# A bidirectional hybrid encoder: a fourth seven-product pair per gate/up group, and half of the lower weight halves made by accumulating DMA

## The chip, the cores and the metric

One core of a Trainium2 chip runs the whole kernel in one launch. The metric is device time in microseconds, the median of three runs; lower is better. A profiled execution of the same program gives the page and the trace.

## The reference

Two layers over 256 tokens of width 2048, in float32. Each layer mixes tokens (layer 0 by a chunked gating unit, layer 1 by grouped-query attention with a 2-D rotary embedding), attends to 256 memory tokens, and then runs a dense SwiGLU feed-forward network of width 5632:

```python
x = x + jnp.concatenate([tok_out, mem_out], axis=-1) @ w_out[l]
x = x + swiglu(rms_norm(x, g_ffn[l]), w_gate_up[l], w_down[l])

def swiglu(h, w_gate_up, w_down):
    gate, up = jnp.split(h @ w_gate_up, 2, axis=-1)
    return (jax.nn.silu(gate) * up) @ w_down
```

The gate/up weights are 2 x 2048 x 11264 numbers, the down weights 2 x 5632 x 2048. All weights are read once from HBM.

## The kernel before, in words

**Three matmuls for one product.** Every operand is split into a rounded upper half and the remainder, both in the type fp32r. A product is three matmuls (`matmul3`, L185 to L189): upper x upper, lower x upper, upper x lower. Each has 128 x 128 stationary numbers (activations, turned) and 128 x 512 moving ones (weights), and adds into a PSUM bank.

**Splitting the weights.** A raw tile (tag `raw`, four slots, 128 x 4 x 512, 1 MB) comes in by two transfers of 512 KB from SyncE's queue. `halves` (L265) makes from it `whi` by a cast on ScalarE (L271) and `wlo` = raw - whi on VectorE (L272). There are three slots each of `whi` and `wlo`.

**Groups and pairs.** The gate/up projection of a layer goes in 11 groups of 512 gate and 512 up columns (class `Pair`, L333). A group takes two column blocks (gate, up) by two blocks of 128 tokens, and walks through the 2048 rows in eight pairs of 128-row blocks. An ordinary pair (`eight`, L409) makes eight products, 24 matmuls. A fast pair (`seven`, L395) gets the same result from seven products, 21 matmuls, in the manner of Strassen and Winograd: sums of activations are made once per layer (`feature_sums`), and sums of weights for each pair in `prepare` (L362): the tile `T` of three blocks by L371 and L373, and one block of `raw` overwritten by L372. `T` then goes through `halves` as well (L397, 128 x 1536). Products 1, 5, 6, 7 add up in four banks of their own (`banks2`), the others in four `acc` banks. After the last fast pair `inner` (L421) evicts the four special banks to a tile `E` (L425 to L428). After the last pair `outer` (L443) adds the `acc` banks to it, and lines 845 to 850 do the SiLU gating and send the result through a transposing DMA (L200 to L206) to the down projection. Groups come in chunks of four, four and three; each is followed by its part of the down projection, which uses the same class with fast pairs of its own.

**What sets the order.** `run` (L350) prepares each pair one ahead, also across the groups of a chunk; `tick` puts due side work in between. The order on each engine is then set by a scheduler from the order of the code and from slots coming free, and each engine runs its list strictly in that order. In the first group of a layer two pairs are fast, in the other ten three. Hence a group has 6 x 24 + 2 x 21 = 186 or 5 x 24 + 3 x 21 = 183 matmuls.

Of the kernel before, what the change touches and what calls it, by code (L numbers as in the profile page):

```python
# [10 lines left out]
F32 = mybir.dt.float32  # L11
# [6 lines left out]
P = 128  # L18
# [13 lines left out]
KC2 = 2  # L32
KC4 = 4
MIX_TILES = 36
FFN_TILES = 26
W_TILES = 3
RAW_TILES = 4
KC3 = 3
# [3 lines left out]
class Parts:  # L42
# [8 lines left out]
    def get(self, kc, t):  # L51
        return self.ap[kc, t]
# [3 lines left out]
def encoder(ctx: ExitStack, tc: tile.TileContext, x, x_t, mem, mem_t, columns, w_in_a, g_v_a, spatial_t, w_in_b,  # L56
# [128 lines left out]
    def matmul3(out, a, b, start, stop):  # L185

        nc.tensor.matmul(out, lhsT=a[0], rhs=b[0], start=start, stop=False)  # L187
        nc.tensor.matmul(out, lhsT=a[1], rhs=b[0], start=False, stop=False)  # L188
        nc.tensor.matmul(out, lhsT=a[0], rhs=b[1], start=False, stop=stop)  # L189
# [75 lines left out]
    def halves(raw, n, step=KC4):  # L265

        hi = wp.tile([P, KC4, NB], F32R, tag="whi", name=nm("whi"))[:, :n]
        lo = wp.tile([P, KC4, NB], F32R, tag="wlo", name=nm("wlo"))[:, :n]
        for c in range(0, n, step):
            cut = slice(c, min(c + step, n))  # L270
            nc.scalar.copy(hi[:, cut], raw[:, cut])  # L271
            nc.vector.tensor_tensor(lo[:, cut], raw[:, cut], hi[:, cut].bitcast(F32), ALU.subtract)  # L272
# [60 lines left out]
    class Pair:  # L333
# [1 line left out]

        def __init__(self, parts, sums, w, na, nb, order, fast, into=None):
            self.parts, self.sums, self.w, self.na, self.nb, self.into = parts, sums, w, na, nb, into  # L340
            self.bank, self.two, self.part, self.ready = {}, {}, {}, {}
            self.order, self.fast = order, fast
# [19 lines left out]
        def prepare(self, i):  # L362
# [5 lines left out]
            if i in self.fast:  # L368
# [4 lines left out]
                nc.vector.tensor_tensor(T[:, 2], raw[:, 0], raw[:, 2], ALU.add)  # L373
                self.ready[i] = raw, T

        def fetch(self, i):
            raw = wp.tile([P, KC4, NB], F32, tag="raw", name=nm("raw"), bufs=RAW_TILES)
            rows = slice(2 * i * P, (2 * i + 2) * P)
            for cut, n0 in ((slice(1, 3), self.na), (slice(0, 4, 3), self.nb)):
                nc.sync.dma_start(raw[:, cut], self.w[rows, n0:n0 + NB].rearrange("(c p) n -> p c n", p=P))  # L380
            return raw

        def add(self, name, a, b):
# [7 lines left out]
            self.part.setdefault(name, 0)  # L391
            self.part[name] += 1
            matmul3(self.bank[name], a, b, self.part[name] == 1, self.part[name] == self.of.get(name, self.most))

        def seven(self, i, raw, T):  # L395
            t2, w00, w10, w11 = halves(raw, KC4)
            t1, t3, t4 = halves(T, KC3)  # L397
            get, (q5, s2, q7, q3) = self.parts.get, self.sums[i]
            k0, k1 = 2 * i, 2 * i + 1
            inner = [(1, get(k0, 0), w00), (6, s2, t2), (5, q5, t1), (7, q7, t3)]  # L400
            outer = [(2, get(k1, 0), w10), (3, q3, w11), (4, get(k1, 1), t4)]
            if self.bank:
                inner, outer = inner[:2] + outer[:2], inner[2:] + outer[2:]
            for some in (inner, outer):
                for name, a, b in some:
                    self.add(name, a, b)
                tick()

        def eight(self, i, raw):  # L409
            done = i == self.order[-1]  # L410
            w01, w00, w10, w11 = halves(raw, 4)
            get, k0, k1 = self.parts.get, 2 * i, 2 * i + 1
            for t, names in ((0, (2, 3)), (1, (4, 8))):
                for name, pair in zip(names, ((w00, w10), (w01, w11))):
                    self.add(name, get(k0, t), pair[0])
                    self.add(name, get(k1, t), pair[1])
                if done:
                    self.outer(t)
                tick()

        def inner(self):  # L421

            b = self.bank
            E = room["p"].tile([P, 4, NB], F32, tag="e", name=nm("e"), bufs=1)
            nc.scalar.copy(E[:, 0], b[1])  # L425
            nc.vector.tensor_tensor(E[:, 3], b[6], E[:, 0], ALU.subtract)
            nc.vector.tensor_tensor(E[:, 1:3], self.two[5, 7], E[:, 3:].to_broadcast([P, 2, NB]), ALU.add)
            nc.vector.tensor_tensor(E[:, 3], b[5], E[:, 2], ALU.add)  # L428
            if self.into:
                for t in range(NT):  # L430
                    later(1 + t, lambda t=t: self.add_inner(E, t))
            self.out = self.into or [[E[:, 2 * t + n] for n in range(2)] for t in range(NT)]
# [7 lines left out]
            else:  # L440
                nc.vector.tensor_tensor(o.whole, o.whole, E[:, :2], ALU.add)

        def outer(self, t):  # L443

            o = self.out
            for n, name in enumerate(((2, 3), (4, 8))[t]):
# [201 lines left out]
    for l in range(DEPTH):  # L648
# [172 lines left out]
        for chunk in (range(0, 4), range(4, 8), range(8, 11)):  # L821
# [103 lines left out]
```

## Time and profile before

| | |
|---|---|
| median of 3 runs (range) | 1997.43 us (1996.91 to 1998.39) |
| profiled execution, its own time | 2000.43 us |
| its span | 1998.7 us |
| TensorE busy | 1987.4 us (99%), clock granted 1.0 |
| VectorE busy | 1595.2 us (80%) |
| ScalarE busy | 1228.9 us (61%) |
| GpSimd busy | 66.4 us (3%) |
| bytes by DMA | 416.48 MB, mean 208 GB/s |

The engines are PE (TensorE matmul), PEld (its weight loads), DVE (VectorE), ACT (ScalarE), POOL (GpSimd) and SP (SyncE, which only issues transfers). A row of instructions gives line, engine, operation, output <- inputs, shapes and count; then busy time in us and the mean ns of one; then the idle time of the engine before them and what ended it. A row of waits gives total us, times and the longest. In the DMA rows a digit is the busy tenths of the 16 DMA engines in one slice of the window, and below it stand the GB/s of the slice. The queue q1 carries SyncE's transfers, q10 those of ScalarE (the transposes), q0 those of GpSimd.

### The profile page before, as it was taken

What the parts mean: (1) busy time and instruction counts of PE and PEld (TensorE: products, weight loads), DVE (VectorE), ACT (ScalarE), POOL (GpSimd) and SP (SyncE); (2) the same over time, 40 slices, a digit from 0 to 9 for tenths busy, and PEclk for the clock granted to TensorE, in tenths of its full rate; (3) what the DMA queues carried; (4) which work ended last, traced back from release to release, by engine and by line L of the source; (5) the groups of instructions that cost most, each with busy time, mean ns of one, the idle gap of its engine ahead of it and who ended that gap; (6) DMA issues with size and microseconds to landing.
All of it is one profiled execution on the core that took longest, in us unless ns stands there. A gap on an engine that the chain in (4) does not pass through costs nothing.

```text
span 1998.7 us, 23974 instructions
## 1 busy us (share of the span) xinstructions
PE 1987.4 (99%) x8956; PEld 1646.0 (82%) x8956; DVE 1595.2 (80%) x1700; ACT 1228.9 (61%) x1476; POOL 66.4 (3%) x106
## 2 busy tenths in 40 slices
PE   9999999999999999999999999999999999999998
PEld 7888888888888878888888888888888888888887
DVE  6665568998888979886666886699988899888887
ACT  8757775676446764466765765756754466644673
POOL 2200001000000000000011000010000000000000
PEclk9999999999999999999999999999999999999999
DMA  9856875676656877657766434757866567765674
GB/s 352 296 187 179 242 212 188 190 231 216 220 197 183 229 201 229 205 184 232 228 219 201 162 129 158 219 180 207 241 205 212 188 206 213 225 219 190 199 220 139
DMA packets 276965, 416.48 MB, mean 208 GB/s; under 512 B 85200, under 2 KB 85456, under 8 KB 276848
## 3 DMA queue, kind: packets, MB, share of 16 engines
q1 hardware_dynamic: 199808, 387.62, 59.6%
q10 hardware_dynamic: 74352, 18.81, 5.8%
q0 software_dynamic: 2688, 8.52, 1.4%
q8 instruction: 70, 1.15, 0.2%
q14 instruction: 47, 0.39, 0.1%
HBM read 394.45 MB, written 2.10 MB: 198 GB/s over the span
## 4 chain that ended last, share of the span: by engine, by line
PE 89%; DVE 4%; DMA 3%; issue 2%; ACT 2%; SPq 0%; ACTq 0%; DVEq 0%
PE acc L189 26%; PE acc L187 26%; PE acc L188 26%; PE m L189 4%; PE m L187 4%; PE m L188 4%; DVE wlo L272 2%; DMA a<-a 1%; ACT whi L271 1%; DMA raw<-in_w_down 1%; DMA raw<-in_w_in_a 1%; PE m L193 1%; DVE T L371 0%; DVE e L448 0%; PE m L542 0%
## 5 line engine op out<-in xcount | busy, mean ns | idle before, releaser
L272 DVE TENSOR_TENSOR wlo<-raw,whi 128x2048 fp32r<-128x2048 f32 (+2 forms) x466 | 840.4, 1819 | 253.1 <-ACT whi L271 235.5
L271 ACT CAST whi<-raw 128x2048 fp32r<-128x2048 f32 (+2 forms) x466 | 705.6, 1535 | 428.5 <-PE acc L188 316.4
L187 PE MATMUL acc<-whi,h 128*128 128x512 f32 x1440 | 561.4, 390 | 0.8 <-ACT whi L271 0.8
L188 PE MATMUL acc<-whi,h 128*128 128x512 f32 x1440 | 561.0, 390 | 0.0
L189 PE MATMUL acc<-wlo,h 128*128 128x512 f32 x1440 | 516.0, 391 | 0.7 <-DVE wlo L272 0.6
L187 PE MATMUL acc<-whi,a 128*128 128x512 f32 x1052 | 410.0, 390 | 3.3 <-DVE x L448 2.1
L188 PE MATMUL acc<-whi,a 128*128 128x512 f32 x1052 | 410.0, 390 | 0.0
L189 PE MATMUL acc<-wlo,a 128*128 128x512 f32 x1052 | 394.4, 390 | 0.2 <-DVE wlo L272 0.2
L189 PEld LDWEIGHTS acc<-wlo,h 128*128 128x128 f32 x1440 | 270.4, 188 | 59.6 <-DVE wlo L272 4.1
L187 PEld LDWEIGHTS acc<-whi,h 128*128 128x128 f32 x1440 | 270.4, 188 | 56.5 <-ACT whi L271 1.5
L188 PEld LDWEIGHTS acc<-whi,h 128*128 128x128 f32 x1440 | 270.4, 188 | 55.7
L187 PEld LDWEIGHTS acc<-whi,a 128*128 128x128 f32 x1052 | 197.6, 188 | 44.7 <-issue 2.5
L189 PEld LDWEIGHTS acc<-wlo,a 128*128 128x128 f32 x1052 | 197.6, 188 | 42.3 <-DVE wlo L272 1.7
L188 PEld LDWEIGHTS acc<-whi,a 128*128 128x128 f32 x1052 | 197.6, 188 | 40.5
L271 ACT CAST whi<-T 128x1536 fp32r<-128x1536 f32 x84 | 124.4, 1481 | 96.3 <-PE acc L188 75.9
L272 DVE TENSOR_TENSOR wlo<-T,whi 128x1536 fp32r<-128x1536 f32 x84 | 146.9, 1749 | 0.0
L371 DVE TENSOR_TENSOR T<-raw 128x1024 f32<-128x1024 f32 x84 | 102.3, 1217 | 26.0 <-DMA raw<-in_w_gate_up 24.0
L189 PE MATMUL m<-wlo,a 128*128 128x512 f32 x272 | 106.1, 390 | 0.2 <-DVE wlo L272 0.2
L187 PE MATMUL m<-whi,a 128*128 128x512 f32 x272 | 106.0, 390 | 0.2 <-ACT whi L271 0.2
L188 PE MATMUL m<-whi,a 128*128 128x512 f32 x272 | 105.9, 389 | 0.0
L206 ACT COPY sg<-a 128x1024 uint16<-128x1024 uint16 x44 | 51.6, 1174 | 54.9 <-DMA a<-a 54.7
L200 ACT COPY a<-sg 128x1024 uint16<-128x1024 uint16 x44 | 45.9, 1044 | 26.0 <-issue 13.2
(122 smaller groups left out, 1474.7 us busy)
## 6 DMA issues: line engine op xcount, KB each, us to landing
raw<-in_w_gate_up SPq DMA_DIRECT2D x352, 512.0 KB, 4.7
raw<-in_w_down SPq DMA_DIRECT2D x176, 512.0 KB, 5.0
raw<-in_w_out SPq DMA_DIRECT2D x32, 1024.0 KB, 5.3
raw<-in_w_in_a SPq DMA_DIRECT2D x24, 1024.0 KB, 6.9
raw<-in_w_in_b SPq DMA_DIRECT2D x24, 1024.0 KB, 5.2
raw<-in_w_mem_kv SPq DMA_DIRECT2D x16, 1024.0 KB, 5.2
a<-in_mem_t POOLq DMA_DIRECT2D x16, 256.0 KB, 3.9
raw<-in_w_in_a SPq DMA_DIRECT2D x7, 512.0 KB, 8.1
```

Source lines behind the costliest of these rows:

```text
L187: nc.tensor.matmul(out, lhsT=a[0], rhs=b[0], start=start, stop=False)
L188: nc.tensor.matmul(out, lhsT=a[1], rhs=b[0], start=False, stop=False)
L189: nc.tensor.matmul(out, lhsT=a[0], rhs=b[1], start=False, stop=stop)
L193: nc.tensor.transpose(dst[:, c * P:(c + 1) * P], src[:, c * P:(c + 1) * P], ident)
L200: nc.scalar.copy(planes.rearrange("p (h n) -> p h n", h=2), src.bitcast(U16).rearrange("p (n h) -> p h n", h=2))
L206: nc.scalar.copy(halves, back.rearrange("p (h n) -> p n h", h=2))
L271: nc.scalar.copy(hi[:, cut], raw[:, cut])
L272: nc.vector.tensor_tensor(lo[:, cut], raw[:, cut], hi[:, cut].bitcast(F32), ALU.subtract)
L371: nc.vector.tensor_tensor(T[:, :2], raw[:, 1:4:2], w01, ALU.add)
```

## The change

In the ten later gate/up groups of each layer four pairs are fast instead of three, in the order 0, 4, 1, 2, 5, 3, 6, 7 (fast: 0 to 3). In all 22 gate/up groups half of each raw tile gets its lower halves in another way (`added`): ScalarE casts the raw blocks to `whi` (L388) and writes their rounded negation to `wlo` (L389), and a DMA issued by GpSimd adds the raw numbers to that (L390). In a fast pair the source is the raw tile in SBUF, in an ordinary pair it is HBM once more. The other half goes the old way, in instructions of half the size. The matmuls that need the accumulated halves are put last in their pair (`late`). `E` loses its own buffer and takes one of the four raw slots; the memory goes to the pool of activations (26 to 30 tiles), which holds the sums of the fourth pair. The down projection has the new place of `E` but no accumulating DMA.

```diff
-FFN_TILES = 26
+FFN_TILES = 30
...
         def fetch(self, i):
             raw = wp.tile([P, KC4, NB], F32, tag="raw", name=nm("raw"), bufs=RAW_TILES)
...
+            apart = i in self.fast or not self.dma
+            for cut, n0 in ((slice(1, 3) if apart else slice(0, 2), self.na),
+                            (slice(0, 4, 3) if apart else slice(2, 4), self.nb)):
+                nc.sync.dma_start(raw[:, cut], self.block(i, n0))
             return raw
 
+        def added(self, raw, hi, lo, source):
+
+            nc.scalar.copy(hi, raw)
+            nc.scalar.mul(lo, raw, -1.0)
+            nc.gpsimd.dma_start(lo, source, accum_op=ALU.add)
...
+            self.term(name, a[0], b[0])
+            self.term(name, a[1], b[0])
+            if late is None:
+                self.term(name, a[0], b[1])
+            else:
+                late.append((name, a[0], b[1]))
...
         def seven(self, i, raw, T):
-            t2, w00, w10, w11 = halves(raw, KC4)
+            if self.dma:
+                hi = wp.tile([P, KC4, NB], F32R, tag="whi", name=nm("whi"))
+                lo = wp.tile([P, KC4, NB], F32R, tag="wlo", name=nm("wlo"))
+                self.added(raw[:, 2:], hi[:, 2:], lo[:, 2:], raw[:, 2:])
+                nc.scalar.copy(hi[:, :2], raw[:, :2])
+                nc.vector.tensor_tensor(lo[:, :2], raw[:, :2], hi[:, :2].bitcast(F32), ALU.subtract)
+                t2, w00, w10, w11 = [(hi[:, c], lo[:, c]) for c in range(KC4)]
...
-            outer = [(2, get(k1, 0), w10), (3, q3, w11), (4, get(k1, 1), t4)]
+            outer = [(4, get(k1, 1), t4), (2, get(k1, 0), w10), (3, q3, w11)]
...
+            late = [] if self.dma else None
             for some in (inner, outer):
                 for name, a, b in some:
-                    self.add(name, a, b)
+                    self.add(name, a, b, late if name in (2, 3) else None)
+                if some is outer:
+                    for term in late or ():
+                        self.term(*term)
                 tick()
...
+        def eight_added(self, i, raw):
+            done = i == self.order[-1]
+            hi = wp.tile([P, KC4, NB], F32R, tag="whi", name=nm("whi"))
+            lo = wp.tile([P, KC4, NB], F32R, tag="wlo", name=nm("wlo"))
+            self.added(raw[:, 2:], hi[:, 2:], lo[:, 2:], self.block(i, self.nb))
+            nc.scalar.copy(hi[:, :2], raw[:, :2])
+            nc.vector.tensor_tensor(lo[:, :2], raw[:, :2], hi[:, :2].bitcast(F32), ALU.subtract)
+            late = {}
+            for n in range(2):
+                for t in range(NT):
+                    name = ((2, 3), (4, 8))[t][n]
+                    late[t] = [] if n else None
+                    for c in range(2):
+                        self.add(name, self.parts.get(2 * i + c, t), (hi[:, 2 * n + c], lo[:, 2 * n + c]), late[t])
...
+            for t in range(NT):
+                for name, a, b in late[t]:
+                    self.term(name, a, b)
...
-            E = room["p"].tile([P, 4, NB], F32, tag="e", name=nm("e"), bufs=1)
+            E = wp.tile([P, 4, NB], F32, tag="raw", name=nm("raw"), bufs=RAW_TILES)
...
-        fast = (0, 1, 2)
+        fast = (0, 1, 2, 3)
...
-                order, some = ((3, 4, 5, 0, 6, 1, 7, 2), 2) if f == 0 else ((0, 3, 1, 4, 2, 5, 6, 7), 3)
-                pairs[f] = Pair(hF, sums, w_gate_up[l], f * NB, DFF + f * NB, order, fast[:some])
+                order, some = ((3, 4, 5, 0, 6, 1, 7, 2), 2) if f == 0 else ((0, 4, 1, 2, 5, 3, 6, 7), 4)
+                pairs[f] = Pair(hF, sums, w_gate_up[l], f * NB, DFF + f * NB, order, fast[:some], dma=True)
```

How the built order moves is seen at two places. First ScalarE, in a gate/up group of the first chunk of layer 0. Before, `L271` casts a whole raw tile or a whole `T`:

```order
L271 CAST whi_3577<-raw_3513 128x2048
L271 CAST whi_3581<-T_3516 128x1536
L271 CAST whi_3618<-raw_3574 128x2048
L847 ACTIVATE sg_3568<-e_3431,s_427_2649 128x512
L847 ACTIVATE sg_3571<-e_3431,s_430_2655 128x512
L271 CAST whi_3650<-raw_3611 128x2048
L271 CAST whi_3654<-T_3614 128x1536
```

After, in the same part of a group, `L388` and `L416` or `L456` cast half a tile each, and `L389` writes the negation:

```order
L903 ACTIVATE sg_3663<-raw_3559,s_427_2652 128x512
L903 ACTIVATE sg_3666<-raw_3559,s_430_2658 128x512
L416 CAST whi_3672<-raw_3605 128x1024
L271 CAST whi_3679<-T_3608 128x1536
L388 CAST whi_3716<-raw_3669 128x1024
L456 CAST whi_3716<-raw_3669 128x1024
L389 ACTIVATE wlo_3717<-raw_3669 128x1024
L388 CAST whi_3755<-raw_3709 128x1024
L416 CAST whi_3755<-raw_3709 128x1024
L389 ACTIVATE wlo_3756<-raw_3709 128x1024
```

A raw tile takes three instructions on ScalarE in place of one, and the gating (`L903`) now reads a raw slot.

Second TensorE, in the second chunk of layer 0, an ordinary pair. Before, the first matmul that needs `wlo` stands eight behind the pair's first one:

```order
L187 MATMUL acc_5385<-whi_5472,h_2464 128x512
L188 MATMUL acc_5385<-whi_5472,h_2465 128x512
L187 MATMUL acc_5389<-whi_5472,h_2464 128x512
L188 MATMUL acc_5389<-whi_5472,h_2465 128x512
L187 MATMUL acc_5393<-whi_5472,h_2487 128x512
L188 MATMUL acc_5393<-whi_5472,h_2488 128x512
L187 MATMUL acc_5426<-whi_5472,h_2487 128x512
L188 MATMUL acc_5426<-whi_5472,h_2488 128x512
L189 MATMUL acc_5385<-wlo_5473,h_2464 128x512
```

After, the pair of tiles `whi_5618` and `wlo_5619` begins with these rows, whose `wlo` numbers are the half that VectorE makes:

```order
L409 MATMUL acc_5599<-whi_5618,h_2487 128x512
L409 MATMUL acc_5599<-whi_5618,h_2488 128x512
L409 MATMUL acc_5262<-wlo_5515,h_2605 128x512 x2
L409 MATMUL acc_5297<-wlo_5515,h_2636 128x512 x2
L409 MATMUL acc_5603<-wlo_5575,h_2132 128x512
L409 MATMUL acc_5603<-whi_5618,h_2464 128x512
```

and its accumulated half is read 45 matmuls behind the first of these rows, after most of the next pair's matmuls (tiles 5657, 5658, 5664, 5665):

```order
L409 MATMUL m_5592<-whi_5664,a_2716 128x512
L409 MATMUL m_5592<-whi_5664,a_2717 128x512
L409 MATMUL m_5592<-wlo_5665,a_2716 128x512
L409 MATMUL acc_5606<-wlo_5619,h_2464 128x512 x2
L409 MATMUL acc_5641<-wlo_5619,h_2487 128x512 x2
L409 MATMUL acc_5606<-whi_5657,a_2716 128x512
L409 MATMUL acc_5606<-whi_5657,a_2717 128x512
```

Those four matmuls read what the accumulating transfer has written. The program has 176 such transfers on GpSimd's queue, and 60 matmuls fewer than before.

More of the change, by code (lines that the diff above doesn't have):

```diff
@@ L333, in encoder, with __init__ @@
     class Pair:
-        def __init__(self, parts, sums, w, na, nb, order, fast, into=None):
+        def __init__(self, parts, sums, w, na, nb, order, fast, into=None, dma=False):
             self.parts, self.sums, self.w, self.na, self.nb, self.into = parts, sums, w, na, nb, into
             self.bank, self.two, self.part, self.ready = {}, {}, {}, {}
-            self.order, self.fast = order, fast
+            self.order, self.fast, self.dma = order, fast, dma
             some = [i for i in order if i in fast]
@@ L374, in prepare, with block, add @@
                 self.ready[i] = raw, T
+        def block(self, i, n0):
+            return self.w[2 * i * P:(2 * i + 2) * P, n0:n0 + NB].rearrange("(c p) n -> p c n", p=P)
         def fetch(self, i):
             raw = wp.tile([P, KC4, NB], F32, tag="raw", name=nm("raw"), bufs=RAW_TILES)
-            rows = slice(2 * i * P, (2 * i + 2) * P)
-            for cut, n0 in ((slice(1, 3), self.na), (slice(0, 4, 3), self.nb)):
-                nc.sync.dma_start(raw[:, cut], self.w[rows, n0:n0 + NB].rearrange("(c p) n -> p c n", p=P))
-            return raw
-        def add(self, name, a, b):
+            apart = i in self.fast or not self.dma
+            for cut, n0 in ((slice(1, 3) if apart else slice(0, 2), self.na),
+                            (slice(0, 4, 3) if apart else slice(2, 4), self.nb)):
+                nc.sync.dma_start(raw[:, cut], self.block(i, n0))
+            return raw
+        def added(self, raw, hi, lo, source):
+            nc.scalar.copy(hi, raw)
+            nc.scalar.mul(lo, raw, -1.0)
+            nc.gpsimd.dma_start(lo, source, accum_op=ALU.add)
+        def add(self, name, a, b, late=None):
             if name not in self.bank:
@@ L390, in add, with term @@
                     self.bank[name] = psa.tile([P, NB], F32, tag="acc", name=nm("acc"))
-            self.part.setdefault(name, 0)
-            self.part[name] += 1
-            matmul3(self.bank[name], a, b, self.part[name] == 1, self.part[name] == self.of.get(name, self.most))
-        def seven(self, i, raw, T):
-            t2, w00, w10, w11 = halves(raw, KC4)
+            self.term(name, a[0], b[0])
[4 more added lines that the diff above has]
+                late.append((name, a[0], b[1]))
+        def term(self, name, a, b):
+            n = self.part[name] = self.part.get(name, 0) + 1
+            nc.tensor.matmul(self.bank[name], lhsT=a, rhs=b, start=n == 1, stop=n == 3 * self.of.get(name, self.most))
+        def seven(self, i, raw, T):
+            if self.dma:
[5 more added lines that the diff above has]
+                t2, w00, w10, w11 = [(hi[:, c], lo[:, c]) for c in range(KC4)]
+            else:
+                t2, w00, w10, w11 = halves(raw, KC4)
             t1, t3, t4 = halves(T, KC3)
@@ L419, in eight @@
                 tick()
+        def eight_added(self, i, raw):
[12 more added lines that the diff above has]
+                        self.add(name, self.parts.get(2 * i + c, t), (hi[:, 2 * n + c], lo[:, 2 * n + c]), late[t])
+                    if done and not n:
+                        self.outer(t, (0,))
+                if not n:
+                    tick()
+            for t in range(NT):
+                for name, a, b in late[t]:
+                    self.term(name, a, b)
+                if done:
+                    self.outer(t, (1,))
+            tick()
         def inner(self):
             b = self.bank
-            E = room["p"].tile([P, 4, NB], F32, tag="e", name=nm("e"), bufs=1)
+            E = wp.tile([P, 4, NB], F32, tag="raw", name=nm("raw"), bufs=RAW_TILES)
             nc.scalar.copy(E[:, 0], b[1])
@@ L441, in add_inner, with outer @@
                 nc.vector.tensor_tensor(o.whole, o.whole, E[:, :2], ALU.add)
-        def outer(self, t):
+        def outer(self, t, some=(0, 1)):
             o = self.out
-            for n, name in enumerate(((2, 3), (4, 8))[t]):
+            for n in some:
+                name = ((2, 3), (4, 8))[t][n]
                 op = ALU.subtract if name == 4 and not self.into else ALU.add
```

2 lines of the change are left out of this document (added).

## The prediction, made before the changed kernel had run

> **What bounds the kernel now.** First the page: span and busy shares, then how long the chain of work is on each engine.
>
> ```profile
> span 1998.7 us, 23974 instructions
> PE 1987.4 (99%) x8956; PEld 1646.0 (82%) x8956; DVE 1595.2 (80%) x1700; ACT 1228.9 (61%) x1476; POOL 66.4 (3%) x106
> PE 89%; DVE 4%; DMA 3%; issue 2%; ACT 2%; SPq 0%; ACTq 0%; DVEq 0%
> ```
>
> TensorE works for 1987.4 of 1998.7 us. Only 11.3 us could be won by filling its gaps; more has to come from fewer matmuls. What a matmul costs is the distance between starts, not the 390 ns of its row, since matmuls overlap. The timeline of TensorE inside a gate/up group, first and last of 42 rows in a row:
>
> ```profile
> 429.70 0.39 PE L187 MATMUL acc<-whi,h 128*128 128x512 f32 x1
> ...
> 438.99 0.39 PE L187 MATMUL acc<-whi,h 128*128 128x512 f32 x1
> ```
>
> 41 distances in 9.29 us are 0.2266 us each. A group holds 3 x 21 + 5 x 24 = 183 matmuls, 41.5 us. The timeline of ScalarE has the same beat, since this copy comes once in a group:
>
> ```profile
> 415.62 0.58 ACT L425 COPY e<-m 128x512 f32<-128x512 f32 x1
> ...
> 457.10 0.58 ACT L425 COPY e<-m 128x512 f32<-128x512 f32 x1
> ```
>
> Next, what the others do meanwhile: the table of stages for 40 us of one group, and the waits there.
>
> ```profile
> core 0: us, PE busy (x) PEld busy (x) DVE busy (x) ACT busy (x) POOL busy (x), PEclk, DMA share, GB/s
> 390.00:430.00 40.00, 40.00 (x178) 33.11 (x177) 38.10 (x36) 27.58 (x23) 0.00 (x0) 1.00 0.72 219
> ```
> ```profile
> ACT whi L271 <- PE acc L188: 11.0, 4, 4.0
> DVE wlo L272 <- ACT whi L271: 1.9, 2, 1.3
> ```
>
> VectorE is busy 38.10 of 40 us and TensorE still loses nothing. So a helper at 95% is affordable here, but another seven-product pair cannot be paid by VectorE as it stands. ScalarE waits mostly for TensorE to give buffers back.
>
> **The change, part by part.**
>
> *Products.* Twenty of the 22 groups (the first of each layer keeps two) change one eight-product pair into a seven-product one: 20 x 3 = 60 matmuls x 0.2266 = **13.6 us** off TensorE. A group becomes 180 x 0.2266 = 40.8 us. This is the most that the change can bring.
>
> *VectorE and ScalarE.* The groups of instructions, by form:
>
> ```profile
> L272 DVE TENSOR_TENSOR wlo<-raw,whi 128x2048 fp32r<-128x2048 f32 x264 | 603.3, 2286 | 138.1 <-ACT whi L271 121.7 <-DMA raw<-in_w_down 15.5 <-DMA raw<-in_w_gate_up 0.9
> L271 ACT CAST whi<-raw 128x2048 fp32r<-128x2048 f32 x264 | 505.1, 1914 | 349.7 <-PE acc L188 253.8 <-DVE raw L372 36.5 <-PE m L188 20.9
> L272 DVE TENSOR_TENSOR wlo<-raw,whi 128x1024 fp32r<-128x1024 f32 x198 | 234.5, 1221 | 114.1 <-ACT whi L271 112.9 <-PE m L193 0.7
> L271 ACT CAST whi<-raw 128x1024 fp32r<-128x1024 f32 x198 | 198.2, 1048 | 77.8 <-PE acc L188 62.6 <-DMA raw<-in_w_in_a 8.7 <-issue 6.3
> L272 DVE TENSOR_TENSOR wlo<-T,whi 128x1536 fp32r<-128x1536 f32 x84 | 146.9, 1749 | 0.0
> L271 ACT CAST whi<-T 128x1536 fp32r<-128x1536 f32 x84 | 124.4, 1481 | 96.3 <-PE acc L188 75.9 <-DVE T L373 13.3 <-DVE raw L372 7.0
> L371 DVE TENSOR_TENSOR T<-raw 128x1024 f32<-128x1024 f32 x84 | 102.3, 1217 | 26.0 <-DMA raw<-in_w_gate_up 24.0 <-DMA raw<-in_w_down 1.7
> L372 DVE TENSOR_TENSOR raw<-T,raw 128x512 f32<-128x512 f32 x84 | 57.1, 681 | 0.0
> L373 DVE TENSOR_TENSOR T<-raw 128x512 f32<-128x512 f32 x84 | 57.1, 681 | 0.1
> ```
>
> VectorE, per group: the eight 2.29 become eight 1.22 (-8.6 us); the fourth combination adds 1.22 + 0.68 + 0.68 + 1.75 = 4.3 us. So 38 becomes about 34 of 40.8 us. ScalarE: eight 1.91 (15.3) become two casts of 1.05 and one negation of the same size, taken at 1.05 since no row shows it, so 8 x 3.15 = 25.2; the fourth T cast adds 1.48. With the 27.58 of the stage that is 27.58 + 9.9 + 1.5, near 39 us, less some 1.5 us in which successive instructions overlap: **37.5 of 40.8 us, 92%**. That is where VectorE stands today without harm, so I cost it at nothing; the cover gone, it is rival C.
>
> *The accumulating transfers.* 176 new transfers of 512 KB, eight in a group, issued by GpSimd, whose own part of an issue the groups of instructions give:
>
> ```profile
> L594 POOL DMA_DIRECT2D a<-in_mem_t x16 | 9.2, 574 | 5.0 <-PE m L189 3.0 <-DMA a<-in_spatial_t 1.4 <-POOL a L148 0.3
> L158 POOL DMA_DIRECT2D a<-in_rope_c x1 | 0.8, 789 | 672.5 <-DVE h L232 672.5
> ```
>
> 0.57 to 0.79 us, so eight times 0.8 in 40.8 us on an engine that is otherwise idle there: 0. An issue that waits for its negation holds up only later issues of the same kind and the few norm scalars. What counts is the 16 DMA engines, which the loads of the raw weights use. The DMA view of the same 40 us:
>
> ```profile
> DMA  6000000379999898999999930179934899799569
> GB/s 260 0 0 0 0 0 0 35 195 406 393 249 147 302 244 190 373 218 330 393 391 373 389 109 0 12 127 379 408 123 55 272 399 334 164 397 399 113 168 395
> q1 hardware_dynamic: 4254, 8.19, 64.9%
> q10 hardware_dynamic: 2112, 0.52, 6.8%
> raw<-in_w_gate_up SPq DMA_DIRECT2D x16, 512.0 KB, 4.6
> ```
>
> Full slices (digit 9) reach 373 to 408 GB/s; I take 400. A load of 512 KB (0.524 MB) then fills all engines for 1.31 us, and sixteen of them for 21.0 us of a group. The transposes take 6.8% of 40 us, 2.7 us. No row shows an accumulating transfer. Lower bound: it costs what a load costs, 1.31 us. Upper bound: today's mean, 64.9% of 40 us over 16 loads, 1.62 us, twice: 3.24 us. It must fetch 512 KB of source and 512 KB of destination before it writes. A load is one fetch and one write and already keeps the engines full, so I take two loads, 2.62 us, eight times 21.0 us. Sum: 21.0 + 2.7 + 21.0 = **44.7 us of DMA for 40.8 us of TensorE**. The break-even price is (40.8 - 23.7) / 8 = 2.14 us. Half of the sources come from HBM again, half from SBUF; I price them alike.
>
> The Trainium skill (Collectives: The Full Stack, "The bandwidth ceiling: the fold count and why AG ≠ RS ≠ AR") says that an adding transfer is slower because both operands are read through the same ring, 62.28 against 32.35 GB/s. By that ratio of 1.93 an accumulate is 2.53 us and the group 43.9 us, an estimate; no run here shows it yet. The Trainium skill (DMA: Bandwidth & Descriptors, "Where 436 GB/s comes from") puts the ceiling at 435 GB/s; at that rate 16 loads and 16 fetches would be 38.6 us, the group 41.3 us by an estimate, and the time about rival B's. The trace's full slices stay at 373 to 408, and the measurement decides.
>
> *Waiting for them.* The page's rows on time from issue to landing:
>
> ```profile
> raw<-in_w_gate_up SPq DMA_DIRECT2D x352, 512.0 KB, 4.7
> a<-in_mem_t POOLq DMA_DIRECT2D x16, 256.0 KB, 3.9
> a<-in_mem POOLq DMA_DIRECT2D x8, 256.0 KB, 8.2
> ```
>
> In the new order of TensorE the matmuls that need the accumulated half of an eight-product pair stand 45 matmuls behind its first one: 10.2 us. From a free buffer to landed data I count a negation (1.05), an issue (0.8) and 4 to 8 us: 6 to 10 us. With quiet queues it fits and costs nothing; with full ones it does not.
>
> *Banks in raw slots.* In the timeline of VectorE the last reader of the evicted banks of that group is:
>
> ```profile
> 438.27 0.74 DVE L848 SCALAR_TENSOR_TENSOR sg<-e,s,sg 128x512 f32<-128x512 f32 x1
> ```
>
> From the copy at 415.62 they now hold one of the four raw slots for some 23 us of a group. Three slots at 5.1 us each still span 15 us, against 4.7 us of landing and about 7 us of sums and casts: 0. Bounds: 0, and 3 us in each of 20 groups, 60 us, should an accumulate keep a slot for 8 us. The same in the down projection, where nothing is accumulated, I cost at 0.
>
> *Sum.* Gate/up today is 20 x 41.5 + 2 x 42.2 = 914 us; bound by DMA it is 22 x 44.7 = 983 us: +69 us. Against the profiled execution (2000.43 us, 1.7 us of it outside the span) that gives 2069; against the median, 3 us lower, **2066 us**. At 410 GB/s the group is 43.7 us and the time 2044; with engines 4% idle between full slices it is 46.6 us and 2108. This case alone: 2040 to 2110.
>
> **Rivals.**
>
> *A, faster: the second fetch is nearly free.* Fetching the destination from SBUF may overlap with the source's. Then eight cost 10.5 us, DMA is at 34.2 of 40.8 us, and TensorE stays the bound: 1997.4 - 13.6 = 1984 us, up to 1992 with some stalls. For it: 28% of the engines' time is free today (DMA share 0.72), and helpers at 95% do no harm. Against it: full slices already come in runs of several us, and each accumulate waits in the same queues. It decides at a price below 2.14 us.
>
> *B, a price of 2.0 us* (by bytes in and out, 1.5 times a load): 21.0 + 2.7 + 16.0 = 39.7 us, 97% of TensorE's 40.8. Late transfers then take 0 to 1.5 us of a group, 0 to 33 us in all: 1984 to 2017, centre 1998.
>
> *C, ScalarE or the buffers.* Accumulates are cheap, but negations stand in ScalarE's order in front of casts that TensorE needs, and ScalarE is at 92%. One to three us of a group lost: -13.6 + 22 to 66, 2006 to 2050.
>
> That the change leaves the matmuls in is excluded: the program has 60 fewer.
>
> **How the numbers follow.** Forecast 0.50, A 0.30, B 0.13, C 0.07. The measurement resolves about 0.2%, 4 us. Faster: A and 0.03 of B, 0.33. Same: 0.06 of B and 0.02 of C, 0.08. Slower: the forecast, 0.04 of B and 0.05 of C, 0.59. The range reaches from A's end to the forecast's upper end, 1983 to 2110; about 0.15 is left out, some of it above (3.24 us a piece) and some below.
>
> **What would show it.** Right: in gate/up stages a DMA share of 0.95 or more, TensorE near 40 us of 44 with waits on the accumulated lower halves or on raw loads, landings of 512 KB loads well over 4.7 us, ScalarE below 90%. Wrong: a pitch of the bank copies near 40.8 us and TensorE at 40 of 40 (A); waits on ScalarE's casts at a DMA share below 0.9 (C).

## The result, and the profile after

The changed kernel takes 2315.19 us (median of four runs, 2301.01 to 2325.82), the kernel before 1997.91 us (four runs, 1996.91 to 2003.49): a ratio of 1.158, 95% interval [1.151, 1.164]. The forecast was 2066 us. The direction was right and the size was not: +317 us in place of +69.

The page of the changed kernel, its span and busy shares, the DMA engines, two queues and the landings:

```profile
span 2312.1 us, 24997 instructions
PE 2070.3 (90%) x8896; PEld 1663.4 (72%) x8896; DVE 1523.6 (66%) x1794; ACT 1441.8 (62%) x1850; POOL 244.3 (11%) x282
...
DMA  9767879997699966899866346799967999769984
...
q1 hardware_dynamic: 199808, 387.62, 51.6%
q0 software_dynamic: 39808, 100.81, 23.2%
...
raw<-in_w_gate_up SPq DMA_DIRECT2D x352, 512.0 KB, 6.6
...
wlo<-in_w_gate_up POOLq DMA_DIRECT2D x92, 512.0 KB, 9.4
wlo<-raw POOLq DMA_DIRECT2D x84, 512.0 KB, 8.7
```

TensorE has its 60 matmuls fewer (8896 for 8956) and is yet busy for 82.9 us more. A load of 512 KB now lands after 6.6 us, before 4.7. An accumulate takes 9.4 us from HBM and 8.7 us from SBUF. Next the stages: four stretches of gate/up, then one of the down projection.

```profile
core 0: us, PE busy (x) PEld busy (x) DVE busy (x) ACT busy (x) POOL busy (x), PEclk, DMA share, GB/s
330.00:380.00 50.00, 37.61 (x151) 28.77 (x149) 28.15 (x32) 29.71 (x30) 7.18 (x7) 0.94 0.97 242
380.00:430.00 50.00, 45.65 (x187) 35.84 (x187) 36.48 (x42) 38.57 (x43) 8.39 (x8) 0.96 0.94 239
430.00:480.00 50.00, 34.81 (x141) 27.44 (x140) 26.82 (x34) 28.79 (x33) 7.19 (x7) 0.86 1.00 204
480.00:530.00 50.00, 36.76 (x136) 26.81 (x135) 28.00 (x29) 28.30 (x29) 5.74 (x6) 0.86 1.06 203
580.00:630.00 50.00, 50.00 (x222) 41.40 (x221) 40.63 (x36) 26.37 (x20) 3.01 (x3) 1.00 0.68 222
```

In gate/up the DMA engines are at 0.94 to 1.06, VectorE and ScalarE are busy for 54 to 77% of the time, and TensorE stands still for 4 to 15 of 50 us. In the third and fourth rows the granted clock falls to 0.86: 136 matmuls fill 36.76 us there, where 36.76 us held 162 before. This stretch of the down projection, without accumulates, is whole. The waits of TensorE, the five longest rows:

```profile
PE acc L409 <- DMA wlo<-raw: 87.4, 32, 13.3
PE acc L409 <- DMA wlo<-in_w_gate_up: 35.6, 25, 4.4
PE acc L409 <- DVE wlo L457: 33.4, 12, 4.4
PE acc L409 <- ACT whi L271: 24.9, 9, 7.7
PE m L409 <- ACT whi L416: 23.8, 8, 5.4
```

All rows of that view add up to 236 us, before to 7. That makes the account of the span: 229 us more waiting, 13.6 us fewer matmuls, and 96.5 us (2070.3 less 1987.4 - 13.6) by which TensorE is busy for longer with the same matmuls; together 312 of the 313.4 us between the spans. Of the 96.5 us some 62 are the clock: by the trace's clock records it stood at one half for 180.9 us, and in 124.3 of these TensorE was at work. The others are mostly matmuls whose successor came late, which count with the 0.39 us of their row in place of 0.2266. The timeline across the longest wait shows how a late landing is passed on:

```profile
425.39 1.86 ACTq L201 DMA_TRANSPOSE a<-a  x1
427.57 0.86 POOL L390 DMA_DIRECT2D wlo<-raw  x1 [9.27 <-DVE wlo L417]
...
445.12 1.16 ACT L206 COPY sg<-a 128x1024 uint16<-128x1024 uint16 x1 [11.62 <-DMA a<-a]
446.19 1.05 ACT L389 ACTIVATE wlo<-raw 128x1024 fp32r<-128x1024 f32 x1
...
447.39 0.79 PE L409 MATMUL acc<-wlo,h 128*128 128x512 f32 x1 [13.28 <-DMA wlo<-raw]
...
447.53 0.91 POOL L390 DMA_DIRECT2D wlo<-raw  x1 [14.54 <-ACT wlo L389]
...
447.98 0.63 PE L409 MATMUL acc<-wlo,a 128*128 128x512 f32 x1
...
448.41 1.05 PE L409 MATMUL acc<-whi,h 128*128 128x512 f32 x2
```

TensorE stood for 13.28 us until the accumulate issued at 427.57 had landed, 19.8 us after its issue. ScalarE stood for 11.62 us before a copy that needs the transpose issued at 425.39; a load issued at 426.76 landed 18.2 us later. So three kinds of transfer were late together, while the DMA engines were held all the time and moved little:

```profile
432.00:436.00 4.00, 2.11 (x10) 1.42 (x8) 2.04 (x3) 1.50 (x2) 0.99 (x1) 1.00 0.97 53
436.00:440.00 4.00, 0.00 (x0) 0.00 (x0) 0.00 (x0) 0.00 (x0) 0.00 (x0) 0.82 1.01 64
```

Why they moved only 53 to 64 GB/s there is not shown; this is the longest of 121 waits. The negation comes right behind the copy in ScalarE's fixed order, so the next accumulate is issued only at 447.53, after GpSimd stood for 14.54 us. The matmuls after TensorE's gap start 0.43 us apart (447.98, 448.41) in place of 0.2266.

### The profile page after: what moved, and what is told of

Same layout as the page of the kernel before. It is cut to its first block, busy times and chain, and to the rows that moved or that the text cites. A ratio compares the mean times of both kernels' runs of the same rounds, so it can differ in the third digit from the quotient of the medians.

```text
span 2312.1 us, 24997 instructions
## 1 busy us (share of the span) xinstructions
PE 2070.3 (90%) x8896; PEld 1663.4 (72%) x8896; DVE 1523.6 (66%) x1794; ACT 1441.8 (62%) x1850; POOL 244.3 (11%) x282
## 3 DMA queue, kind: packets, MB, share of 16 engines
q1 hardware_dynamic: 199808, 387.62, 51.6%
## 5 line engine op out<-in xcount | busy, mean ns | idle before, releaser
L272 DVE TENSOR_TENSOR wlo<-raw,whi 128x1024 fp32r<-128x1024 f32 (+2 forms) x290 | 436.7, 1537 | 164.2 <-ACT whi L271 161.3
L409 PE MATMUL acc<-whi,h 128*128 128x512 f32 x1808 | 528.9, 406 | 2.0 <-ACT whi L271 2.0
L271 ACT CAST whi<-raw 128x1024 fp32r<-128x1024 f32 (+2 forms) x290 | 367.2, 1304 | 235.4 <-PE acc L409 76.4
L409 PE MATMUL acc<-whi,a 128*128 128x512 f32 x1376 | 412.6, 398 | 29.8 <-ACT whi L271 23.0
L409 PEld LDWEIGHTS acc<-whi,h 128*128 128x128 f32 x1808 | 357.8, 198 | 81.4 <-ACT whi L271 2.8
L409 PEld LDWEIGHTS acc<-whi,a 128*128 128x128 f32 x1376 | 262.3, 192 | 91.4 <-ACT whi L271 26.7
L388 ACT CAST whi<-raw 128x1024 fp32r<-128x1024 f32 x176 | 184.3, 1047 | 139.7 <-PE acc L409 80.2
L409 PE MATMUL acc<-wlo,a 128*128 128x512 f32 x688 | 250.4, 397 | 9.5 <-DVE wlo L272 9.5
L272 DVE TENSOR_TENSOR wlo<-T,whi 128x1536 fp32r<-128x1536 f32 x104 | 182.6, 1756 | 51.6 <-ACT whi L271 37.2
L390 POOL DMA_DIRECT2D wlo<-in_w_gate_up x92 | 111.1, 1207 | 900.1 <-ACT wlo L389 736.7
L389 ACT ACTIVATE wlo<-raw 128x1024 fp32r<-128x1024 f32 x176 | 185.4, 1056 | 31.9 <-PE acc L409 31.9
L271 ACT CAST whi<-T 128x1536 fp32r<-128x1536 f32 x104 | 153.2, 1473 | 56.7 <-PE acc L409 39.2
L187 PE MATMUL acc<-whi,h 128*128 128x512 f32 x416 | 162.4, 392 | 1.6 <-ACT whi L271 1.6
L188 PE MATMUL acc<-whi,h 128*128 128x512 f32 x416 | 162.2, 390 | 0.0
L390 POOL DMA_DIRECT2D wlo<-raw x84 | 76.2, 907 | 725.6 <-ACT wlo L389 614.3
```

The costliest lines, as they stand in the source:

```text
L388: nc.scalar.copy(hi, raw)
L389: nc.scalar.mul(lo, raw, -1.0)
L390: nc.gpsimd.dma_start(lo, source, accum_op=ALU.add)
L409: nc.tensor.matmul(self.bank[name], lhsT=a, rhs=b, start=n == 1, stop=n == 3 * self.of.get(name, self.most))
```

## The experiments

The theory after the two traces: the accumulates cost about what was forecast in DMA time, and the rest is late landings that are passed on by few buffers and fixed orders. The rivals: a higher price beside other transfers; the banks in raw slots; four fast pairs in a group; ScalarE's longer list. All ratios are to the kernel before, timed on the same chip, with their 95% intervals; "+us" is the difference of the medians. Gaps are all waits of TensorE in one profile, added up; busy is its busy time there.

| run | kernel | ratio [interval] | gaps, us | PE busy, us |
|---|---|---|---|---|
| before | | 1 | 7 | 1987.4 |
| after | | 1.158 [1.151, 1.164] | 236 | 2070.3 |
| 1 | after, plain copy | 1.079 [1.076, 1.083] | 119 | 2035.5 |
| 2 | after, no transfer | 1.038 [1.035, 1.040] | 64 | 1994.8 |
| 3 | after, accumulates in fast pairs only | 1.075 [1.071, 1.079] | 103 | 2031.9 |
| 4 | after, old split | 1.078 [1.075, 1.080] | 107 | 2032.0 |
| 5 | before, banks in a raw slot | 1.029 [1.025, 1.032] | 44 | 2009.8 |
| 6 | three pairs, negation, no transfer | 1.000 [0.999, 1.001] | 5 | 1985.2 |
| 7 | three pairs, all accumulates | 1.121 [1.117, 1.124] | 170 | 2067.3 |
| 8 | run 4, fast pairs spread | 1.073 [1.069, 1.076] | 102 | 2040.3 |
| 10 | run 7, plain transfers | 1.023 [1.021, 1.026] | 39 | 2000.6 |
| 11 | run 7, fast pairs only (3 a group) | 1.036 [1.034, 1.039] | 55 | 2011.1 |
| 12 | run 11, sources from HBM | 1.045 [1.043, 1.048] | 66 | 2015.8 |
| 13 | run 7, all sources from HBM | 1.126 [1.120, 1.132] | 177 | 2060.3 |
| 14 | run 7, ordinary pairs only (5 a group) | 1.098 [1.096, 1.100] | 121 | 2061.3 |
| 15 | run 7, transfers of 256 KB | 1.067 [1.065, 1.069] | 98 | 2029.2 |
| 16 | run 14, no transfer | 1.011 [1.010, 1.013] | 20 | 1996.8 |
| 17 | run 15, no transfer | 1.000 [0.999, 1.001] | 6 | 1986.6 |
| 18 | run 14, result not read | 1.084 [1.082, 1.086] | 107 | 2050.9 |

### Which part costs it: the changed kernel less one piece

Run 1 lets the same transfers go without adding:

```diff
-            nc.gpsimd.dma_start(lo, source, accum_op=ALU.add)
+            nc.gpsimd.dma_start(lo, source)
```

> The changed kernel with the GpSimd transfers as plain copies of the same bytes: nothing is added, so the accumulated half of the lower halves holds the raw numbers. All other instructions stay. Theory D (demand: the second fetch of each accumulate fills the DMA engines): one fetch is about 1.35 us, a group needs 21.5 + 10.8 + 2.7 = 35 us of DMA against 40.8 us of TensorE, so 1984 to 2000 us and a DMA share near 0.85. Theory Q (queueing: the engines are not full, but long landings of accumulates and transposes hold up engines that run in order): a third queue still delays the transposes, 2030 to 2120 us. Theory S (the extra ScalarE work and the bank in a raw slot cost the time): above 2250 us.

It took 2157.12 us, above the ranges of D and Q and below that of S. Run 2 leaves the transfer out altogether (that line is deleted).

> The changed kernel without the GpSimd transfers: the accumulated half keeps the bare negation. D and Q: nothing delays TensorE any more, 60 matmuls less than before, 1984 to 1992 us, clock 1.0, ScalarE near 92% in gate/up. S: ScalarE at 92% with the bank in a raw slot stalls TensorE, 2050 us or more.

It took 2072.65 us. So the changed kernel without any transfer is 73 us slower than before, the plain transfers add 84, and adding in them another 158. Run 3 keeps the accumulates of the fast pairs alone:

```diff
-            apart = i in self.fast or not self.dma
+            apart = True
...
-            if self.dma:
-                return self.eight_added(i, raw)
```

> The accumulating DMA only in the seven-product pairs (84 transfers, all from SBUF); the eight-product pairs split the whole raw tile on ScalarE and VectorE as before. D: four transfers of 2.62 us leave a group at 21.5 + 10.5 + 2.7 = 34.7 us of DMA, and VectorE at about 39 of 40.8 us, so 1985 to 2010 us. Q: landings of accumulates in the seven-product pairs still stall TensorE and lower its clock, about half of the loss, 2080 to 2170 us. S: 2150 us or more.

It took 2148.86 us. Run 4 has four fast pairs and the banks in raw slots, but the old split:

```diff
-..., order, fast[:some], dma=True)
+..., order, fast[:some])
```

> Four seven-product pairs and the bank in a raw slot, but all lower halves by VectorE, no accumulating DMA. VectorE gets 4.3 us more in a group, 38.1 + 4.3 = 42.4 against 40.8 us of TensorE: 20 groups of 42.4 instead of 41.5 us, 2005 to 2025 us under D and Q. S, if the bank in a raw slot is the trouble: 2050 us or more.

It took 2154.22 us, 155 us more than before, and slower than run 2: the new split without its transfers takes half of that away. Run 8 asks whether the neighbouring fast pairs do it:

```diff
-... ((0, 4, 1, 2, 5, 3, 6, 7), 4)
+... ((0, 4, 1, 5, 2, 6, 3, 7), 4)
```

> Four fast pairs with the old split and the bank in a slot, in the order 0, 4, 1, 5, 2, 6, 3, 7, so that no two fast pairs follow each other. S2 in the form that two fast pairs in a row need four sets of halves from three buffers: 2040 to 2100 us instead of 2154. S1, or VectorE's total: 2130 us or more.

It took 2146.5 us: the order isn't the cause. Four pairs with a buffer of their own for the banks were not tried.

### Banks in raw slots, alone

Run 5 is the kernel before with this edit only:

```diff
-            E = room["p"].tile([P, 4, NB], F32, tag="e", name=nm("e"), bufs=1)
+            E = wp.tile([P, 4, NB], F32, tag="raw", name=nm("raw"), bufs=RAW_TILES)
```

> The kernel before with one line changed: the evicted banks take a raw slot instead of a buffer of their own. Theory S1 (the slot: with three raw slots for half a group the loads come late): most of the 155 us of the four-pair kernel with the old split, so 2080 us or more, with waits on raw loads. Theory S2 (the fourth pair: more lower halves for VectorE and more tiles through three buffers): 1995 to 2005 us, no difference.

It took 2058.85 us, between the two expectations. A wait of ScalarE's and one of VectorE's before, and then the same two in run 5:

```profile
ACT whi L271 <- DVE raw L372: 43.5, 8, 9.5
...
DVE T L371 <- DMA raw<-in_w_gate_up: 24.0, 13, 3.7
```
```profile
ACT whi L271 <- DVE raw L372: 187.3, 42, 10.7
...
DVE T L371 <- DMA raw<-in_w_gate_up: 14.7, 14, 2.0
```

With three slots left VectorE makes the sums later, and the cast that stands behind them in ScalarE's order waits 42 times in place of 8. VectorE itself waits no longer for raw data than before (14.7 against 24.0 us). So late loads are not seen to hold the sums up there; whether the order of VectorE's list does, or the wait for a free slot, was not separated.

### The split without and with the transfers, in the old frame

Runs 6, 7 and 10 have three fast pairs and the banks in their own buffer, and change the split only. Run 6 has casts and negations, but no transfer:

```diff
+            nc.scalar.copy(hi, raw)
+            nc.scalar.mul(lo, raw, -1.0)
```

> Three fast pairs and an own buffer for the banks as before; half of the lower halves is the bare negation by ScalarE, with no transfer adding to it (that half of the numbers is left wrong). It holds the extra ScalarE work and the lighter VectorE alone. Theory S3 (the negations on ScalarE stall TensorE): 2030 us or more. S1 and S2: 1995 to 2003 us.

It took 1999.6 us, as before. With three fast pairs ScalarE's new work costs nothing, though it is at 41 to 42 of 50 us:

```profile
330.00:380.00 50.00, 50.00 (x220) 40.90 (x219) 36.87 (x43) 42.10 (x46) 0.00 (x0) 1.00 0.65 208
380.00:430.00 50.00, 50.00 (x222) 41.40 (x221) 39.38 (x47) 41.32 (x47) 0.00 (x0) 1.00 0.70 232
```

Run 7 adds the accumulating transfer behind those two lines.

```diff
+            nc.gpsimd.dma_start(lo, source, accum_op=ALU.add)
```

> Three fast pairs, an own buffer for the banks, and the accumulating DMA in all pairs: the transfers alone. If costs add up, the 83 us of a plain copy and the 158 us of the second fetch come on top of before: 2200 to 2260 us. If DMA demand alone sets the pace (46 us against 41.5 us of TensorE): 2080 to 2110 us.

It took 2242.99 us. Run 10 is run 7 with run 1's edit, plain transfers.

> Three fast pairs, own buffer for the banks, and the GpSimd transfers as plain copies, so that half of the lower halves holds the raw numbers. P1: 25.7 + 8 x 1.5 + 3.6 = 41 us of DMA against 41.5 us of TensorE, 2000 to 2030 us. P2: clean demand is 35 us, but landings grow and TensorE waits, 2040 to 2090 us.

It took 2046.83 us. The stages of run 7, and then of run 10:

```profile
330.00:380.00 50.00, 39.59 (x155) 30.57 (x154) 28.06 (x30) 32.13 (x34) 7.55 (x7) 0.93 0.92 231
380.00:430.00 50.00, 42.12 (x166) 33.52 (x165) 29.62 (x36) 32.48 (x36) 8.03 (x8) 0.90 0.92 236
```
```profile
330.00:380.00 50.00, 46.43 (x204) 37.82 (x203) 34.42 (x38) 41.23 (x45) 5.47 (x9) 1.00 0.88 277
380.00:430.00 50.00, 49.22 (x216) 40.10 (x216) 35.93 (x45) 40.29 (x45) 6.61 (x10) 1.00 0.96 313
```

The busy share is about the same (0.92, and 0.88 to 0.96), the work done is not: 155 and 166 matmuls against 204 and 216. The accumulates add 243 us here, from run 6 to run 7, and 243 us from run 2 to the changed kernel. So in total they cost the same with and without the fourth pair and the banks in raw slots, and those two are the other 73 us. The parts of the 243 us aren't the same, though: plain transfers add 47 us here and 84 there, the adding 196 here and 158 there.

### The price of a transfer

Run 9 has no matmuls, only transfers of 512 KB: loads; plain copies SBUF to SBUF; accumulates from SBUF; a load and an accumulate from HBM in turn.

```python
nc.gpsimd.dma_start(total, raw)                       # L82
nc.gpsimd.dma_start(total, raw, accum_op=ALU.add)     # L85
nc.gpsimd.dma_start(total, block, accum_op=ALU.add)   # L88, from HBM
```

> A kernel that only moves data, so its output is not the encoder's: 64 loads of 512 KB as the gate/up loads; then 32 GpSimd transfers of 512 KB from SBUF to SBUF as plain copies, 32 accumulating from SBUF, 32 accumulating from HBM; then 64 loads together with 32 accumulates from HBM. Theory P1 (demand: at load the engines need the mean packet time, with its long packets): loads alone 1.6 us each, the mixed stage 64 x 1.6 + 32 x 2.9 = 195 us. Theory P2 (queueing: the engines could do more, late landings lose the time): loads 1.33 us, plain copies 1.35, accumulates 2.6 to 2.8, the mixed stage 64 x 1.33 + 32 x 2.7 = 171 us.

```profile
20.00:60.00 40.00, 0.00 (x0) 0.00 (x0) 1.00 1.05 388
105.94:130.96 25.02, 1.10 (x7) 9.51 (x19) 1.00 1.12 389
170.56:205.68 35.12, 1.25 (x8) 10.97 (x13) 1.00 1.06 199
252.52:292.56 40.04, 0.00 (x0) 11.81 (x10) 1.00 1.10 261
```

The last column gives the rates: 388 GB/s is 1.35 us for a load; 18 copies in 25.02 us are 1.39 us each; 13 accumulates in 35.12 us are 2.70 us each; ten pairs of a load and an accumulate in 40.04 us are 4.00 us each, so the accumulate there costs 2.65. From HBM without loads beside them accumulates land 2.55 us apart (seven from 298.61 to 313.89 us). Beside loads an accumulate thus costs some 0.1 us more than by itself.

Run 9 has neither matmuls nor transposes, but the queues of whole kernels can be compared. These are the two of before; those of the changed kernel stand above:

```profile
q1 hardware_dynamic: 199808, 387.62, 59.6%
...
q0 software_dynamic: 2688, 8.52, 1.4%
```

The packets of SyncE's loads took 59.6% of 1998.7 us, 1191 us, before, and 51.6% of 2312.1, 1193 us, after: they got no longer. GpSimd's queue went from 28 to 536 us, 2.89 us for each of 176 accumulates; in run 9 thirteen in 35.12 us at a share of 1.06 are 2.86 us each. With both, the rival of a higher price in the kernel falls. A group of run 7 therefore asks for 16 x 1.35 + 8 x 2.65 + 2.7 = 45.5 us of DMA for 41.5 us of TensorE: 22 x 4.0 = +88 us. Measured are +243.

### Below the bound by demand

Runs 11 to 15 ask for less DMA than TensorE's 41.5 us, or move the source. Run 11 is run 7 with run 3's edit: three accumulates a group, 32 us of demand.

> Three fast pairs, own buffer for the banks, and the accumulating DMA only in the fast pairs, three in a group, all from SBUF; the other five pairs split the whole tile on ScalarE and VectorE. P1: 25.7 + 3 x 2.7 + 3.6 = 37 us of DMA against 41.5, so 1998 to 2010 us. P2: three eighths of the loss of 243 us, 2060 to 2100 us.

It took 2070.65 us. Its accumulates read the raw slot, and SyncE's next load waited for that:

```profile
SPq L383 <- DMA wlo<-raw: 456.8, 64, 11.1
```

Run 12 takes that away, since the same numbers come from HBM:

```diff
-                self.added(raw[:, 2:], hi[:, 2:], lo[:, 2:], raw[:, 2:])
+                self.added(raw[:, 2:], hi[:, 2:], lo[:, 2:], self.again(i))
...
+        def again(self, i):
+            step = (self.nb - self.na) // NB
+            cols = self.w[(2 * i + 1) * P:(2 * i + 2) * P, :].rearrange("p (c n) -> p c n", n=NB)
+            return cols[:, self.na // NB:self.nb // NB + 1:step]
```

> Three fast pairs a group, their accumulates only (three a group), as in the run that gave 1.036 of before; but the numbers to be added come from HBM once more, not from the raw slot, so that the slot is free as soon as ScalarE and VectorE have read it. DMA demand stays at 16 x 1.35 + 2.7 + 3 x 2.55 = 32 of 41.5 us. Theory H (raw slots held until the accumulate has landed, 456.8 us of waits in SyncE's queue): the +73 falls to 0 to +25 us, 2000 to 2025. Theory L (late landings themselves and fuller queues): it stays at +60 to +90, 2060 to 2090.

2088.91 us, slower than run 11; TensorE's waits for the accumulates grew from 14.4 to 36.6 us. Run 13 is run 7 with that edit.

> Three fast pairs, all eight accumulates a group, all from HBM (before: three of them from the raw slot, 1.121 of before, +243 us). Demand 16 x 1.35 + 2.7 + 8 x 2.55 = 44.7 us a group, 22 x 3.2 = +70 us by demand alone. Theory H: the held slots were the rest, 2065 to 2160. Theory L: 2220 to 2260.

2246.45 us, as run 7. The wait for the held slot is gone in both and the lost time isn't: theory H falls as the main cause. Run 14 is run 7 with accumulates in the ordinary pairs only:

```diff
-            if self.dma:
+            if False:
                 hi = wp.tile([P, KC4, NB], F32R, tag="whi", name=nm("whi"))
...
-            late = [] if self.dma else None
+            late = None
```

> Three fast pairs, accumulates only in the five ordinary pairs of a group, from HBM, with the late matmuls 45 behind; the fast pairs are split as before. Demand 16 x 1.35 + 2.7 + 5 x 2.55 = 37 of 41.5 us. Theory D (the larger of the two demands sets a group): 1998 to 2018. Theory C (the cover of the fast pairs, whose late matmuls stand at the end of the same pair, was too short; that of the ordinary ones suffices): 2000 to 2040. Theory L: some 5/8 of +243, 2100 to 2180.

2195.09 us, +197, at a demand of 37 us. Theories D and C fall: these are the pairs with the long cover, and they cost more than the fast ones. Run 15 is run 7 with one block a transfer:

```diff
-                self.added(raw[:, 2:], hi[:, 2:], lo[:, 2:], raw[:, 2:])
+                self.added(raw[:, 3:], hi[:, 3:], lo[:, 3:], raw[:, 3:])
...
-            self.added(raw[:, 2:], hi[:, 2:], lo[:, 2:], self.block(i, self.nb))
+            self.added(raw[:, 3:], hi[:, 3:], lo[:, 3:], self.block(i, self.nb)[:, 1:])
```

> Three fast pairs, eight accumulates a group of 256 KB each, one block of four; VectorE makes three of four blocks. Demand 16 x 1.35 + 2.7 + 8 x 1.33 = 35 of 41.5 us. Theory D: 1998 to 2015. Theory L: about half of +243, 2090 to 2140; landings of 256 KB some 6 us. If the pitch of a group falls out of line with the bytes, the number of transfers counts, not their size: over 2150.

2133.17 us, +135. By bytes accumulated in a group: 1.5 MB cost 73 and 90 us, 2 MB 135, 2.5 MB 197, 4 MB 243 and 248. That rises over the whole range measured, and 73 us are lost at a demand of 32 us already: there is no threshold at 41.5 us. These numbers hold the form of each run as well (the split into halves and the order of the late matmuls); what it costs in runs 11 and 12 was not run.

### Landing, reading, and what the form itself costs

Runs 16 and 17 are 14 and 15 with the transfer's line deleted.

> The kernel with accumulates in the five ordinary pairs only (1.098 of before, +197 us), without the transfers: the lower half keeps the negation. It shows what the split of the halves and the order of the late matmuls cost by themselves. Theory L (the transfers cost all of it, through late landings): 1995 to 2010. Theory O (the order and the half-size instructions of this form cost a good part): 2040 to 2120.

> The kernel with eight accumulates of 256 KB (1.067 of before, +134 us), without the transfers: the quarter keeps the negation. Theory L: 1995 to 2010. Theory O: 2030 to 2090.

Run 16 took 2022.87 us, +23, between the two expectations; run 17 took 1998.88 us, as before. So of run 14's +197 the transfers carry 172 to 174, of run 15's +135 all. Run 18 is run 14 with its transfers, but the late matmuls read something else:

```diff
-                late.append((name, a[0], b[1]))
+                late.append((name, a[0], b[0]))
```

> The kernel with accumulates in the five ordinary pairs only (1.098 of before, +197 us), but no matmul reads what they write: the four late matmuls of a pair and term read the upper half once more in place of the accumulated half. The transfers run as before, and a buffer is still held until its transfer has landed. Theory W (TensorE waits for the landing itself): 2000 to 2040. Theory B (the held buffers, and loads and transposes that come later, carry it): 2140 to 2200.

2167.97 us: of the transfers' 173 us, 145 remain when nobody reads their result, and reading it costs some 27. (Run 18 also holds `whi` for longer and `wlo` for less long, so the split isn't exact.) A count of waits would have said otherwise. In run 14 this row is half of TensorE's 121 us of gaps:

```profile
PE acc L409 <- DMA wlo<-in_w_gate_up: 59.9, 46, 2.9
```

In run 18 the row is gone, and 107 us of gaps remain: TensorE meets the same delays at other waits. What waits then can be seen beside run 16, which has no transfers. A row of VectorE's and one of ScalarE's, of run 16:

```profile
DVE T L370 <- DMA raw<-in_w_gate_up: 30.7, 34, 2.3
```
```profile
ACT sg L206 <- DMA a<-a: 37.6, 35, 4.5
```

and of run 18:

```profile
DVE T L370 <- DMA raw<-in_w_gate_up: 131.8, 38, 7.5
```
```profile
ACT sg L206 <- DMA a<-a: 75.8, 27, 6.8
...
ACT wlo L389 <- DMA wlo<-in_w_gate_up: 43.1, 17, 5.7
```

Loads of raw weights, transposes, and `wlo` buffers whose accumulate has not landed come late, each by up to 7.5 us at a time; the longest landing of a load goes from 8.0 us in run 16 to 13.1 in run 18. TensorE's own waits in run 18 are on VectorE and ScalarE, but for one of 1.4 us. What share each of the three has wasn't separated.

## Why the prediction was wrong

- **Products: right.** The count of matmuls is 60 lower.
- **ScalarE at 92% for nothing: not shown at 92%.** Run 6 is level with before, with ScalarE at 83 to 84% and three fast pairs. With four, in run 2, ScalarE is at 87% at most, and 37 of TensorE's 64 us of waits there are on ScalarE, though the banks hold a raw slot too. Rival C, as a cause by itself, falls: 243 of the 317 us go with the transfers.
- **The price of an accumulate: right.** 2.62 us were taken, 2.55 to 2.70 measured (run 9). The ratio to a plain copy is 2.70 / 1.39 = 1.94. The Trainium skill's 1.93 for a collective (Collectives: The Full Stack, "The bandwidth ceiling: the fold count and why AG ≠ RS ≠ AR") agrees with that. A plain stream reached 388 GB/s here, not the 435 GB/s of the Trainium skill (DMA: Bandwidth & Descriptors, "Where 436 GB/s comes from"). Rivals A and B fall by their price.
- **That DMA's demand alone sets the length of a group: this step failed.** It was the sum's form: 22 x 44.7 us in place of TensorE's time, and nothing added for waiting ("with quiet queues it fits and costs nothing"). The prediction itself named full queues and priced them at zero. Run 7 has the forecast demand and costs 243 us where demand gives 88; run 14 has demand below TensorE's and costs 172 us by its transfers. Landings of 4 to 8 us were taken; they were 9.4 and 8.7, at most 19.8. In run 14 the reading of the accumulated numbers is worth only some 27 of 173 us (run 18); the rest came with late loads, transposes and buffers, passed on by engines in a fixed order.
- **The cover of the fast pairs was left out.** The 10.2 us were worked out for an ordinary pair. By the edit a fast pair's late terms stand at the end of its own 21 matmuls, at most 19 behind its first one, 4.3 us, which is less than the 6 to 10 us that the prediction counted from a free buffer to landed data. In the changed kernel 123 of TensorE's 236 us of waits end with an accumulate's landing, 87 of them in fast pairs. What reading costs there was not run; without the fast pairs' accumulates run 13's 2246 us become run 14's 2195.
- **The row of full slices was read too kindly.** Of the 19 slices with digit 9, 13 moved 373 to 408 GB/s and six only 147 to 334. That a held DMA engine may move little stood in that row already. The price of a load came out right all the same (1.31 us taken, 1.35 in run 9).
- **Banks in raw slots at 0, with bounds of 0 and 60 us: the value failed, the bound held by luck.** Run 5 measures 59 us. The 60 us were meant for an accumulate that keeps a slot, and run 5 has none. That step compared averages (three slots of 5.1 us against a landing of 4.7 and 7 us of use), as did the sum. With the fourth pair and its sums, run 2 is at +73, although 13.6 us of matmuls are gone.
- **The granted clock was not in the sum at all.** It was 1.0 before, so every matmul was priced at 0.2266 us. In the changed kernel some 62 of the 313 us are matmuls at half the clock. The Trainium skill (TensorE: Matmul & The Clock Gate, "HAM oscillation — how this bites in real kernels") says that waiting for a DMA long enough, more than some 3.4 us, throttles TensorE back to half rate; 0.43 us a matmul after a gap of 13.28 us agrees. The traces differ in the length: gaps of 1.8 us did it too (last section). The prediction did not weigh this.

What the prediction named as signs of being right came true (DMA at 0.94 to 1.06 for 0.95 or more, landings over 4.7 us, ScalarE below 90%) except one: TensorE near 40 us of 44, which is 45 of 50. It was 35 to 46 of 50. A share of 0.95 shows that the DMA engines hold packets, not that a group ends when the demand is through: run 10 is at 0.88 to 0.96 and loses 49 us.

## What to carry to other kernels

Where TensorE is at 99% and buffers are few, the larger of two average demands is a lower bound, not a forecast: add what later landings do to every other transfer that shares the engines, even at a demand below the limit. Price a longer transfer by what it does to its neighbours in a run with its result unread. A wait that ends with a landing doesn't show that the landing costs that time: take it away in a run and see what remains. And when gaps are to be expected in TensorE, add the matmuls at half clock behind them: here some 62 us to 229 us of gaps.

## What the hardware showed that was not expected

- Gaps far shorter than the longest one halve the clock. The clock records of the sixteen kernels in which it fell (the changed one and runs 1 to 5, 7, 8, 10 to 16 and 18) hold 232 falls to one half. In each trace they start on a grid of steps of 3.41 us and last one to four steps. The clock fell after every step in which TensorE had stood still for more than 1.93 us in all, and after none in which it had for less than 1.68; in 138 of the 232 no single gap reached 3.4 us. Run 14 has only two gaps above 3.4 us, but 24 falls.
- The busy share of the DMA engines doesn't tell their work: alone, plain copies and accumulates both read 1.06 to 1.12, at 389 and 199 GB/s (run 9; the view counts an accumulate's bytes once).
- At a like demand accumulates hurt more than plain transfers: run 15 (16 x 1.35 + 2.7 + 8 x 1.33 = 35 us of 41.5) costs 135 us, run 10 (16 x 1.35 + 2.7 + 8 x 1.39 = 35.4 us) 49 us, though loads land after 5.5 and 5.8 us in the two, and the form of both costs nothing without its transfers (runs 6 and 17). Why is open.
- GpSimd's part of an issue was 0.53 us in the median for a plain copy, 0.85 for an accumulate from SBUF and 1.18 from HBM (run 9).
